# Output projection of a streaming trunk layer: branch sums on VectorE, branch tiles in another order, transposes of m sooner

## The chip, the cores and the metric

The kernel runs on one core of a Trainium2 chip. Its engines are TensorE (PE, the matmuls; PEld is its weight load), VectorE (DVE), ScalarE (ACT), GpSimd (POOL) and SyncE (SP, which issues most loads and stores). Each engine works through its own list of instructions in order, and waits on semaphores for the others. The metric is the device time of one execution, in microseconds (us). The kernel before took 2628.94, 2624.07 and 2617.74 us in three runs, so its median is 2624.07 us.

## The reference

One layer over 2048 rows of 1024 values. All of it is in float32.

```python
xn = rmsnorm(x, norm1_g)
u_pool, zq, zf, zi, zo, zg = split(xn @ w_in)            # 512 wide each, zg 2 x 1024
gates  = sigmoid(zg + b_gate).reshape(B, S, 2, 1024)
ya     = pool_mixer(u_pool, pool_w, pool_scale) @ w_pa   # branch "pa": 512 -> 1024
yb     = hgrn2_mixer(zq, zf, zi, zo, ...) @ w_pb         # branch "pb": 512 -> 1024
merged = gates[:, :, 0] * ya + gates[:, :, 1] * yb
x      = x + merged @ w_o                                # output projection: 1024 -> 1024
x      = x + (silu(gate) * value) @ w_down               # value, gate = conv(rmsnorm(x, norm2_g) @ w_up)
out    = rmsnorm(x, final_g)
```

## The kernel before

**Numbers and tiles.** Every matrix product is made in three matmuls: each operand is split into a rounded part hi and a rest lo (`split`: a cast to hi on ACT at L597, the difference lo on DVE at L598; weights likewise at L205 and L206), and hi*hi, hi*lo and lo*hi are added in PSUM. A tile is 128 x 512. There are 77 such places in SBUF for everything but weights, and 8 banks of PSUM.

**Seven products for eight.** The large products (input projection, output projection "wo", up projection, down projection "dn") take two blocks of 512 rows and two halves of the other dimensions together and use seven products P1 to P7 of sums and differences in place of eight. The two blocks are called the first rows (hf 0) and the second rows (hf 1) here; 1024 rows make a pass, and the program has two passes. The sums and differences of the input of a product are its forms: P1, P2 and P4 take a block as it is, P7, P5, P6 and P3 need a subtraction or an addition each.

**A pass.** In a pass come, on PE: the input projection, with the two mixers as background tasks; branch "pa"; branch "pb"; the output projection; the up projection; the down projection.

**The two branches.** `branch` goes through eight column tiles m in the order M_ORDER = (0, 4, 1, 5, 2, 6, 3, 7). For each m it fetches the gate tiles of m and the next two, gets the weights, and runs one chain of 12 matmuls of 128 x 512 for the first rows and then one for the second rows. In "pa" the inputs are `mixed` (tiles mx0_k of the first rows and mx1_k of the second, k = 0..3), loaded from DRAM by SP at L796 and split by a task; in "pb" they are `oT` (tiles oT0_k and oT1_k). After a chain `evac_a` multiplies the result with its gate on DVE into `ya`; `evac_b` does so into `gl` (L1285 for second rows, L1287 for first rows) and adds `gl` to `ya` on POOL (L1295). When m is 4 or more and the chain was that of the second rows, all four blocks of k = m - 4 are there, and `add_forms` makes the four forms P7, P5, P6, P3 of that k on POOL (L1084) into `yf`. That is 16 additions and 16 forms on POOL in a pass.

**The output projection.** `Rows.run` works through the products in the order P1, P6, P5, P7, P4, P3, P2, with four steps k each (the last steps of some are taken together), and 12 matmuls a step. `make` splits the forms, LEAD = 5 steps ahead of the step that uses them; the first five splits are therefore asked for when P1 begins. Products alternate between two groups of four banks, A and B: P1 and P5 use the same group A, so P5 waits until the 16 additions of P1's results into x (DVE, L1060) have read it.

**Forms of m.** The result x is called m as the input of the up projection. `forms_of("m")` starts two tasks: the first rows are normalised and transposed on PE at once; the second rows are normalised (L640) at once, but their transposes (L646) and the forms made of them (T2, T1, T3, T4; L703, L597, L598) wait until `go_up` is set. `ffn` sets it at the head of the up projection's unit number GO_AT = 5. The up projection begins with four units of P1, P1, P2, P2 for tiles 0 and 1, four more of the same kind for tiles 2 and 3, and then P6, the first that needs T2.

**What sets the order.** Weights come through `Stream`: raw tiles in 8 buffers (SP, L182), converted to `ops` up to four ahead. A raw load is queued on SP where the program reaches it and waits there for its buffer, and what is queued on SP behind it waits too. After every six matmuls `tick` advances the stream and the tasks by a step, so that background work is interleaved with PE's. The program text gives an order; a scheduler that simulates the engines then chooses the final order of each engine's list.

Of the kernel before, what the change touches and what calls it, by code (L numbers as in the profile page):

```python
# [15 lines left out]
ALU = mybir.AluOpType  # L16
AX = mybir.AxisListType

P = 128
SEQ = 2048  # L20
D = 1024
KD = D // P
# [24 lines left out]
OUT = R_OUT, R_OUT_BANK, R_OUT_NEW, R_OUT_ADD  # L47
# [10 lines left out]
M_ORDER = (0, 4, 1, 5, 2, 6, 3, 7)  # L58
# [1 line left out]
N_SLOTS = 77  # L60
N_RUN = 3
N_HEADS = 2
GO_AT = 5
LEAD = 5
X_AT, X_AT2 = 1, 4
GO_IO = (("P2", 1), ("P2", 0))
# [12 lines left out]
def tile_trunk(  # L79
# [16 lines left out]
    pe, act, dve, pool, sp = nc.tensor, nc.scalar, nc.vector, nc.gpsimd, nc.sync  # L96
# [9 lines left out]
    def slot(name, cols=TB, dt=F32):  # L106
        return slots.tile([P, cols], dt, tag="s", name=name, padded_shape=[P, 528])

    def bank(name, cols=512):
        return banks.tile([P, cols], F32, tag="b", name=name, padded_shape=[P, 512])  # L110
# [33 lines left out]
    def mm(*args, **kw):  # L144
        count[1] = pe.matmul(*args, **kw)  # L145
        count[0] += 1
        if count[0] % MM_PER_TICK == 0:
            tick()
# [102 lines left out]
    stream = Stream()  # L251
# [171 lines left out]
    def up_order():  # L423
        heads = [(0, 1), (2, 3), (4, 5)][:N_HEADS]
        res = [(m, p) for ms in heads for p in ("P1", "P2") for m in ms]
        res += [(m, p) for ms in heads for p in ("P6", "P5", "P7", "P4", "P3") for m in ms]

        rest = [(7 * m + 2 * i, m, p) for m in range(2 * N_HEADS, MF)
                for i, p in enumerate(ORDER)]
        return res + [(m, p) for _, m, p in sorted(rest)]  # L430
# [26 lines left out]
    sums = {}  # L457
# [39 lines left out]
    def load_x_tile(b, j):  # L497
        for c in range(2):
            t = slot(f"x{b}_{j}_{c}")
            r = b * TB + j * P  # L500
            sp.dma_start(t, x[r : r + P, 512 * c : 512 * c + 512])
            xt[("x", b), j, c] = t
        ready.add((("x", b), j))
# [97 lines left out]
    def chain_t(ps, w_of, xs, start=True, stop=True):  # L601
        n = len(xs)
        for k in range(n):
            wh, wl = w_of(k)
            xh, xl = xs[k]
            mm(ps, wh, xh, start=start and k == 0, stop=False)
            mm(ps, wh, xl, start=False, stop=False)
            mm(ps, wl, xh, start=False, stop=stop and k == n - 1)
# [185 lines left out]
    def fetch(d, name, eng=sp):  # L794
        t = slot(name)
        eng.dma_start(t, d)  # L796
        return t
# [277 lines left out]
                        step(j, k, ws[n])  # L1075
                stream.used(hold)

    def add_forms(two, forms, k, name, store=lambda p, t: None, sums=True, pin=lambda i: None):

        def comb(p, x0, x1, op):  # L1080
            if (p, k) in forms or x0 is None or x1 is None:
                return
            t = slot(f"{name}_{p}_{k}")
            pin(pool.tensor_tensor(t, x0, x1, op))  # L1084
            forms[p, k] = t
            store(p, t)

        for p, at in (("P1", (1, 0)), ("P2", (1, 1)), ("P4", (0, 1))):
            if (p, k) not in forms and at in two:
                forms[p, k] = two[at]  # L1090
                store(p, two[at])
        if not sums:
            return
        comb("P7", two.get((1, 0)), two.get((0, 0)), ALU.subtract)
        comb("P5", two.get((0, 0)), two.get((0, 1)), ALU.subtract)
        comb("P6", forms.get(("P5", k)), two.get((1, 0)), ALU.subtract)
        comb("P3", forms.get(("P6", k)), two.get((1, 1)), ALU.add)
# [54 lines left out]
    def mixer(b0, forms, late):  # L1152
# [90 lines left out]
        def gate(s, m, hf):  # L1243
            if (s, m, hf) not in gates:
                gates[s, m, hf] = fetch(gd[s, m, hf], f"gl{b0 + hf}_{s}_{m}")
            return gates[s, m, hf]
# [8 lines left out]
        mixed, oT = {}, {}  # L1255
# [8 lines left out]
                    mtask = Task(pa_task())  # L1264

        def branch(key, s, xs, evac, each):
            for n, m in enumerate(M_ORDER):
                each(n)
                for m2 in M_ORDER[n : n + 3]:
                    for hf in range(2):  # L1270
                        gate(s, m2, hf)
                w4 = stream.get(key)
                for hf in range(2):
                    ps = bank(f"{key}{b0 + hf}_{m}")
                    chain_t(ps, lambda k: (w4[:, 0, k * P : (k + 1) * P],
                                           w4[:, 1, k * P : (k + 1) * P]),
                            [xs[hf, k] for k in range(4)])
                    evac(m, hf, gate(s, m, hf), ps)
                stream.used(1)

        y, yf = {}, {}

        def gated(t, hf, g, ps):
            if hf:
                dve.scalar_tensor_tensor(t, g, -1.0, ps, ALU.mult, ALU.mult)  # L1285
            else:
                dve.tensor_tensor(t, g, ps, ALU.mult)  # L1287
# [4 lines left out]

        def evac_b(m, hf, g, ps):
            gated(g, hf, g, ps)
            pool.tensor_tensor(y[m, hf], y[m, hf], g, ALU.add)  # L1295
            if m >= KD // 2 and hf:
                k = m - KD // 2
                two = {(h, r): y[k + r * (KD // 2), h] for h in range(2) for r in range(2)}
                add_forms(two, yf, k, f"yf{b0}")

        join(mtask)
        otask = []
# [1 line left out]
        def start_o(n):  # L1304
            if n == O_AT:
                otask.append(Task(halves_task(od, range(HEADS), oT, "oT", O_LAG)))

        branch("pa", 0, mixed, evac_a, start_o)
        while any(t.live for t in runners):
            for t in runners:  # L1310
# [4 lines left out]
        acc = {}  # L1315

        def load_res(n):
            hf, j = n // NT, n % NT
            load_x_tile(b0 + hf, j)
            for c in range(2):  # L1320
                acc[hf, j, c] = xt.pop((("x", b0 + hf), j, c))

        branch("pb", 1, oT, evac_b, load_res)

        def ready_rows(hf):
            def done(j):
# [2 lines left out]
                ready.add((("m", b0 + hf), j))  # L1329
            return done  # L1330

        wo = Rows(f"wo{b0}", "wo", OUT, KD // 2, lambda p, k: yf[p, k], acc)
        go_up[0] = False
        for p in ("P1", "P6", "P5"):
            wo.run(p)
# [10 lines left out]
    def ffn(b0, forms, late):  # L1346
# [15 lines left out]
        def emit_up(m):  # L1362
# [17 lines left out]
            def glu(hf):  # L1380
                g = ts[1, hf]
                in_turn(act.activation(g, g, AF.Silu))  # L1382
                if hf:
                    dve.scalar_tensor_tensor(g, g, -1.0, ts[0, hf], ALU.mult, ALU.mult)  # L1384
                else:
                    (pool if m < G_POOL else dve).tensor_tensor(g, g, ts[0, hf], ALU.mult)
                k = m // 2
                two = gp.setdefault(k, {})
                two[hf, m % 2] = g

                def store(p, t):
# [69 lines left out]
        for n, (m, p) in enumerate(up_order()):  # L1461
            if n == GO_AT:
                go_up[0] = True
# [119 lines left out]
```

## Time and profile before

| what | value |
| --- | --- |
| runs | 2628.94, 2624.07, 2617.74 us (median 2624.07) |
| profiled execution | 2626.91 us, span 2625.2 us, mean granted TensorE clock 0.987 |
| PE busy | 2537.5 us (97%) |
| DVE busy | 1977.9 us (75%) |
| ACT busy | 1170.8 us (45%) |
| POOL busy | 913.0 us (35%) |
| POOL: L1295, 32 additions of ya and gl | 46.8 us, mean 1490 ns |
| POOL: L1084 into yf, 32 forms | median 1460 and 1458 ns |

The profile is one execution. PE is busy for 97% of the span, so what an edit can bring lies in the places where PE waits and in those where its granted clock (PEclk, a share of full speed) is low. The view of waits on PE lists them by what PE waited for: total us, how many times, and the longest. The view of windows gives the busy us of each engine in a stretch of time, with the granted clock. In both passes the branch "pb" runs beside POOL's additions; in the first pass "pa" begins at about 490 us and "pb" at 541 us, the output projection at 592 us, the up projection at 683 us; the output projection of the second pass begins at 1873 us.

### The profile page before, as it was taken

The numbers are of one execution on the slowest core, as the hardware profiler recorded it, in microseconds if no ns is written. First come the engines' busy times: TensorE is split into PE (matmuls) and PEld (weight loads), VectorE is DVE, ScalarE is ACT, GpSimd is POOL, SyncE is SP. The second block draws the span as 40 slices with busy tenths as digits, with TensorE's granted clock in tenths as the row PEclk, the third lists the DMA queues.
The fourth block names the chain that finished last, engine by engine and source line by source line (L and its number), as shares of the span: only waits on it lengthen the run. The fifth ranks groups of instructions, "written<-read, shape, count | busy, mean of one in ns | idle before, by whom it ended". The sixth has DMA issues, their size and how long they took to land. (4 is left out here: it accounts for less than half of the span.)

```text
span 2625.2 us, 35598 instructions
## 1 busy us (share of the span) xinstructions
PE 2537.5 (97%) x11464; PEld 2065.1 (79%) x11464; DVE 1977.9 (75%) x3390; ACT 1170.8 (45%) x2204; POOL 913.0 (35%) x1253
## 2 busy tenths in 40 slices
PE   7899999998999999999999999999999999999998
PEld 6688877777778888878878788888787888887887
DVE  7888779458789877877376787775778887777845
ACT  5334334313655454455364344443345454444633
POOL 6544344042444433353141111210623433335402
PEclk8999999999999999999999999999999999999999
DMA  6787759988768897488364344346452444445942
GB/s 213 271 223 205 204 181 245 267 263 209 217 184 244 239 235 211 148 299 282 98 206 159 97 125 133 109 153 213 149 166 88 151 151 148 141 140 182 378 142 105
DMA packets 254059, 496.90 MB, mean 189 GB/s; under 512 B 26736, under 2 KB 43248, under 8 KB 253552
## 3 DMA queue, kind: packets, MB, share of 16 engines
q1 hardware_dynamic: 187968, 319.89, 38.3%
q0 software_dynamic: 41504, 110.64, 16.5%
q10 hardware_dynamic: 24400, 64.08, 7.0%
q8 instruction: 91, 1.49, 0.2%
q14 instruction: 96, 0.79, 0.1%
HBM read 384.94 MB, written 187.17 MB: 218 GB/s over the span
## 5 line engine op out<-in xcount | busy, mean ns | idle before, releaser
L205 ACT CAST ops<-raw 128x512 fp32r<-128x512 f32 x732 | 451.5, 620 | 819.7 <-PE dn_P L145 140.0
L206 DVE TENSOR_TENSOR ops<-raw,ops 128x512 fp32r<-128x512 f32 x732 | 565.2, 776 | 205.3 <-ACT ops L205 194.3
L1375 DVE SCALAR_TENSOR_TENSOR e<-h,cols,e 128x512 f32<-128x512 f32 x176 | 142.6, 813 | 30.2 <-ACT e L1373 26.1
L1373 ACT ACTIVATE e<-h,cols 128x512 f32<-128x512 f32 x176 | 142.5, 814 | 24.2 <-DVE h L978 16.9
L1378 DVE SCALAR_TENSOR_TENSOR e<-h,cols,e 128x512 f32<-128x512 f32 x176 | 133.9, 769 | 3.0
L796 POOL DMA_DIRECT2D g_P<-dg_P x154 | 83.7, 545 | 107.6 <-PE dn_P L145 69.4
L1084 POOL TENSOR_TENSOR gf_P<-e,e 128x512 f32<-128x512 f32 x44 | 67.9, 1545 | 152.9 <-DVE e L1384 97.5
L1295 POOL TENSOR_TENSOR ya<-ya,gl 128x512 f32<-128x512 f32 x32 | 46.8, 1490 | 107.7 <-DVE gl L1287 107.7
L1084 POOL TENSOR_TENSOR gf_P<-gf_P,e 128x512 f32<-128x512 f32 x44 | 60.2, 1368 | 68.0 <-DVE e L1384 67.5
L1368 POOL COPY h<-h 128x2 f32<-128x2 f32 x88 | 40.7, 481 | 114.3 <-DVE h L976 112.3
L1370 POOL COPY hist<-h 128x2 f32<-128x2 f32 x88 | 35.3, 401 | 125.9 <-DVE h L978 124.2
L1382 ACT ACTIVATE e<-e 128x512 f32<-128x512 f32 x88 | 55.6, 631 | 38.8 <-DVE e L1378 38.4
L1191 POOL TENSOR_TENSOR q<-q,qs 128x512 f32<-128x512 f32 x16 | 21.9, 1366 | 141.6 <-ACT qs L1190 72.9
L978 DVE TENSOR_TENSOR h<-up_u,up_V 128x512 f32<-128x512 f32 x88 | 60.1, 684 | 13.6 <-PE up_V L145 13.1
L1228 ACT ACTIVATE gt<-gt,cols 128x512 f32<-128x512 f32 x48 | 34.8, 725 | 77.4 <-DVE gt L978 63.5
L845 POOL COPY qm<-q 128x64 f32<-128x64 f32 x64 | 24.9, 410 | 117.3 <-DVE q L910 31.2
L1060 DVE TENSOR_TENSOR x<-x,wo_P 128x512 f32<-128x512 f32 x88 | 56.6, 689 | 8.2 <-PE wo_P L145 8.2
L1060 DVE TENSOR_TENSOR ac<-ac,dn_P 128x512 f32<-128x512 f32 x72 | 46.6, 684 | 13.4 <-PE dn_P L145 13.3
L1398 POOL DMA_DIRECT2D dg_P<-gf_P x88 | 52.5, 596 | 10.8 <-POOL gf_P L1084 6.5
L853 PE MATMUL pl<-qm,k 128*128 128x192 f32 x256 | 48.2, 331 | 6.1 <-DVE qm L849 3.8
L1444 POOL TENSOR_TENSOR fss<-fss 128x1 f32<-128x1 f32 x16 | 4.6, 288 | 142.0 <-ACT fj L1433 142.0
L853 PEld LDWEIGHTS pl<-qm,k 128*128 128x128 f32 x256 | 43.3, 191 | 10.4 <-ACT qm L844 3.4
(1265 smaller groups left out, 8283.6 us busy)
## 6 DMA issues: line engine op xcount, KB each, us to landing
g_P<-dg_P POOLq DMA_DIRECT2D x154, 256.0 KB, 6.4
raw<-in_w_up_t SPq DMA_DIRECT2D x132, 256.0 KB, 3.2
raw<-in_w_in_t SPq DMA_DIRECT2D x98, 256.0 KB, 3.2
dg_P<-gf_P POOLq DMA_DIRECT2D x88, 256.0 KB, 3.9
raw<-in_w_io SPq DMA_DIRECT2D x68, 256.0 KB, 5.1
dg_P<-e SPq DMA_DIRECT2D x66, 256.0 KB, 3.3
raw<-in_w_dn SPq DMA_DIRECT2D x66, 256.0 KB, 3.0
x<-in_x SPq DMA_DIRECT2D x64, 256.0 KB, 5.3
```

The lines of the kernel that those rows point to most:

```text
L205: self.mark = act.copy(hi, v)
L206: dve.tensor_tensor(lo, v, f32(hi), ALU.subtract)
L796: eng.dma_start(t, d)
L853: pe.matmul(pa_[:, c * 192 : c * 192 + 192], ks[:, (i + c) * P : (i + c + 1) * P], mv[:, c].rearrange("p s x -> p (s x)"), start=True, sto ...
L978: dve.tensor_tensor(dst, t, ps, ALU.add if how == "add" else ALU.subtract)
L1060: dve.tensor_tensor(t, t, ps[j], ALU.add if sg > 0 else ALU.subtract)
L1084: pin(pool.tensor_tensor(t, x0, x1, op))
L1373: in_turn(act.activation(t, h[:, 2:], AF.Identity, bias=col(o_cb + mt), scale=col(o_cw + 4 * MF + mt)))
L1375: in_turn(second(dve.scalar_tensor_tensor(t, h[:, 1 : 1 + TB], col(o_cw + 2 * MF + mt), t, ALU.mult, ALU.add)))
L1378: dve.scalar_tensor_tensor(t, h[:, 0:TB], col(o_cw + mt), t, ALU.mult, ALU.add)
L1382: in_turn(act.activation(g, g, AF.Silu))
L1398: pool.dma_start(d, t)
```

## The change

Four edits:

1. GO_AT goes from 5 to 3, so that the transposes of the second rows of m are let go two units of the up projection sooner.
2. `add_forms` takes the engine as an argument, and `evac_b` uses DVE for the addition of `gl` to `ya` and for the four forms. The 16 + 16 operations of a pass go from POOL to DVE. Other callers of `add_forms` keep POOL.
3. `branch` begins with the first rows of the first two tiles (m = 0, 4), then the second rows of these two, and goes on as before. It holds two weight tiles meanwhile.
4. The Rows object of the output projection is created before branch "pb", and at tiles 3, 5 and 7 of "pb" its first, second and third split (P1, k = 0, 1, 2) are made.

```diff
-GO_AT = 5
+GO_AT = 3
...
-    def add_forms(two, forms, k, name, store=lambda p, t: None, sums=True, pin=lambda i: None):
+    def add_forms(two, forms, k, name, store=lambda p, t: None, sums=True, pin=lambda i: None,
+                  eng=pool):
...
-            pin(pool.tensor_tensor(t, x0, x1, op))
+            pin(eng.tensor_tensor(t, x0, x1, op))
...
         def branch(key, s, xs, evac, each):
-            for n, m in enumerate(M_ORDER):
-                each(n)
-                for m2 in M_ORDER[n : n + 3]:
-                    for hf in range(2):
-                        gate(s, m2, hf)
-                w4 = stream.get(key)
+            ws = {}
+
+            def chain(n, hf):
+                m = M_ORDER[n]
+                if n not in ws:
+                    each(n)
+                    for m2 in M_ORDER[n : n + 3]:
+                        for h in range(2):
+                            gate(s, m2, h)
+                    ws[n] = stream.get(key)
+                w4 = ws[n]
+                ps = bank(f"{key}{b0 + hf}_{m}")
+                chain_t(ps, lambda k: (w4[:, 0, k * P : (k + 1) * P],
+                                       w4[:, 1, k * P : (k + 1) * P]),
+                        [xs[hf, k] for k in range(4)])
+                evac(m, hf, gate(s, m, hf), ps)
+                if hf:
+                    stream.used(1)
+
+
+            for hf in range(2):
+                for n in range(2):
+                    chain(n, hf)
+            for n in range(2, len(M_ORDER)):
                 for hf in range(2):
-                    ps = bank(f"{key}{b0 + hf}_{m}")
...
-                    evac(m, hf, gate(s, m, hf), ps)
-                stream.used(1)
+                    chain(n, hf)
...
         def evac_b(m, hf, g, ps):
             gated(g, hf, g, ps)
-            pool.tensor_tensor(y[m, hf], y[m, hf], g, ALU.add)
+            dve.tensor_tensor(y[m, hf], y[m, hf], g, ALU.add)
             if m >= KD // 2 and hf:
...
-                add_forms(two, yf, k, f"yf{b0}")
+                add_forms(two, yf, k, f"yf{b0}", eng=dve)
...
-        branch("pb", 1, oT, evac_b, load_res)
+        wo = Rows(f"wo{b0}", "wo", OUT, KD // 2, lambda p, k: yf[p, k], acc)
+
+        def each_b(n):
+            load_res(n)
+            if n in (3, 5, 7):
+                wo.make(n // 2)
+
+        branch("pb", 1, oT, evac_b, each_b)
...
-        wo = Rows(f"wo{b0}", "wo", OUT, KD // 2, lambda p, k: yf[p, k], acc)
```

The lines move: L1285, L1287 and L1295 become L1299, L1301 and L1309, and L1084 becomes L1085. How the lists of the engines change shows at three places.

SP in the first pass, between the input projection and branch "pa". mx1_k are the tiles of the second rows, raw125 and raw126 loads of weights. Before:

```order
L796 DMA mx1_0_4864<-md1_0_2260 128x512
L182 DMA raw125_4966<-in_w_pb_t 128x512
L796 DMA mx1_1_4892<-md1_1_2420 128x512
L182 DMA raw126_5020<-in_w_pb_t 128x512
L796 DMA mx1_2_4932<-md1_2_4085 128x512
L796 DMA mx1_3_4938<-md1_3_4203 128x512
```

After:

```order
L796 DMA mx1_0_4864<-md1_0_2260 128x512
L796 DMA mx1_1_4892<-md1_1_2420 128x512
L182 DMA raw125_4966<-in_w_pb_t 128x512
L796 DMA mx1_2_4932<-md1_2_4085 128x512
L182 DMA raw126_4991<-in_w_pb_t 128x512
L796 DMA mx1_3_4938<-md1_3_4203 128x512
```

mx1_1 and mx1_2 each stand ahead of one more weight load; mx1_3 is where it was.

DVE in the first pass, from the last gate of branch "pb" to the first splits of the output projection (ya is the sum of the branches, yf its forms, wo_P_k the splits of a product's step k). Before:

```order
L1287 TENSOR_TENSOR gl_1_7_5586<-gl_1_7_5586,pb_7_5677 128x512
L1285 SCALAR_TENSOR_TENSOR gl_1_7_5588<-gl_1_7_5588,pb_7_5697 128x512
L206 TENSOR_TENSOR ops_5772<-raw_5410,ops_5772 128x512
L598 TENSOR_TENSOR wo_P_0l<-ya_0_5004,wo_P_0h 128x512
L598 TENSOR_TENSOR wo_P_1l<-ya_1_5092,wo_P_1h 128x512
L598 TENSOR_TENSOR wo_P_2l<-ya_2_5195,wo_P_2h 128x512
L598 TENSOR_TENSOR wo_P_3l<-ya_3_5294,wo_P_3h 128x512
L598 TENSOR_TENSOR wo_P_0l<-yf_P_0_5439,wo_P_0h 128x512
```

After:

```order
L1299 SCALAR_TENSOR_TENSOR gl_1_7_5596<-gl_1_7_5596,pb_7_5709 128x512
L206 TENSOR_TENSOR ops_5772<-raw_5390,ops_5772 128x512
L1309 TENSOR_TENSOR ya_7_5319<-ya_7_5319,gl_1_7_5594 128x512
L1309 TENSOR_TENSOR ya_7_5334<-ya_7_5334,gl_1_7_5596 128x512
L206 TENSOR_TENSOR ops_5793<-raw_5461,ops_5793 128x512
L1085 TENSOR_TENSOR yf_P_3_5727<-ya_3_5279,ya_7_5319 128x512
L1085 TENSOR_TENSOR yf_P_3_5729<-yf_P_3_5727,ya_3_5294 128x512
L206 TENSOR_TENSOR ops_5818<-raw_5509,ops_5818 128x512
L1085 TENSOR_TENSOR yf_P_3_5731<-yf_P_3_5729,ya_7_5334 128x512
L598 TENSOR_TENSOR wo_P_3l<-ya_3_5294,wo_P_3h 128x512
L598 TENSOR_TENSOR wo_P_0l<-yf_P_0_5439,wo_P_0h 128x512
```

The splits of P1's steps 0 to 2 are no longer here (they stand in "pb"), and the additions and forms stand ahead of that of step 3.

PE in the first pass, where the transposes of the second rows of m (m_t) come in the up projection. Before, in the middle of the unit P1 of tile 3, the sixth unit of the stage:

```order
L145 MATMUL up_3_X<-m_f1h,ops_6616 128x512
L145 MATMUL up_3_X<-m_f1l,ops_6616 128x512
L145 MATMUL up_3_X<-m_f1h,ops_6616 128x512
L646 MATMUL m_t_6700<-ident,m_xs_0_6459 128x128
L646 MATMUL m_t_6700<-ident,m_xs_0_6509 128x128
L646 MATMUL m_t_6700<-ident,m_xs_0_6542 128x128
L646 MATMUL m_t_6700<-ident,m_xs_0_6581 128x128
```

After, behind the unit P1 of tile 1, the second unit:

```order
L145 MATMUL up_1_X<-m_f3l,ops_6420 128x512
L145 MATMUL up_1_X<-m_f3h,ops_6420 128x512
L646 MATMUL m_t_6660<-ident,m_xs_0_6459 128x128
L646 MATMUL m_t_6660<-ident,m_xs_0_6509 128x128
L646 MATMUL m_t_6665<-ident,m_xs_1_6460 128x128
L646 MATMUL m_t_6665<-ident,m_xs_1_6510 128x128
L646 MATMUL m_t_6688<-ident,m_xs_0_6459 128x128
```

The transposes begin three and a half units sooner, with two of the four row tiles first; the last of the four row tiles comes behind the third unit for the first two columns of tiles, and behind the fourth for the next two.

More of the change, by code (lines that the diff above doesn't have):

```diff
@@ L1266, in branch @@
         def branch(key, s, xs, evac, each):
-            for n, m in enumerate(M_ORDER):
-                each(n)
-                for m2 in M_ORDER[n : n + 3]:
-                    for hf in range(2):
-                        gate(s, m2, hf)
-                w4 = stream.get(key)
-                for hf in range(2):
-                    ps = bank(f"{key}{b0 + hf}_{m}")
-                    chain_t(ps, lambda k: (w4[:, 0, k * P : (k + 1) * P],
-                                           w4[:, 1, k * P : (k + 1) * P]),
-                            [xs[hf, k] for k in range(4)])
-                    evac(m, hf, gate(s, m, hf), ps)
-                stream.used(1)
+            ws = {}
[19 more added lines that the diff above has]
+            for n in range(2, len(M_ORDER)):
+                for hf in range(2):
+                    chain(n, hf)
         y, yf = {}, {}
```

## The prediction, on record before the result was known

> **What bounds the kernel now.** I read the engines' shares first, then the waits on PE, then the windows around the longest of these waits, and last the timelines of the engine that PE waited for.
>
> ```profile
> span 2625.2 us, 35598 instructions
> PE 2537.5 (97%) x11464; PEld 2065.1 (79%) x11464; DVE 1977.9 (75%) x3390; ACT 1170.8 (45%) x2204; POOL 913.0 (35%) x1253
> ```
>
> PE is the bound: only the 88 us in which it does nothing can go, and the time it loses at a low clock. Of the waits on PE these lie in the stages that the change touches (total us, how many, the longest):
>
> ```profile
> PE wo_P L145 <- DVE wo_P_0l L598: 7.3, 2, 6.7
> PE pa L145 <- ACT mxs_1h L597: 6.3, 1, 6.3
> ...
> PE up_Z L145 <- ACT m_T23h L597: 3.7, 2, 1.8
> ...
> PE wo_P L145 <- DVE x L1060: 3.0, 2, 1.6
> ...
> PE wo_P L145 <- ACT wo_P_0h L597: 2.5, 2, 1.2
> ...
> PE pb L145 <- ACT oTs_0h L597: 1.7, 1, 1.7
> ...
> PE up_Z L145 <- DVE m_T23l L598: 1.5, 2, 0.8
> PE up_Z L145 <- ACT ops L205: 1.5, 2, 0.8
> PE up_V L145 <- DVE m_T12l L598: 1.4, 2, 0.7
> ...
> PE pb L145 <- ACT oTs_1h L597: 1.0, 1, 1.0
> ...
> PE up_Z L145 <- DVE up_u L1018: 0.9, 2, 0.5
> ...
> PE up_Z L145 <- DVE m_T43l L598: 0.5, 2, 0.2
> ...
> PE pb L145 <- DVE oTs_1l L598: 0.2, 1, 0.2
> PE pb L145 <- DVE oTs_0l L598: 0.2, 1, 0.2
> ```
>
> That is 6.3 us for pa, 3.1 for pb, 12.8 for wo and 9.5 for up, 31.7 in all. The waits of pa and pb come once, in the first pass; those of wo and up in both. The windows behind the longer ones add a loss (columns: the stretch, its length, busy us of PE, PEld, DVE, ACT, POOL with instructions, granted clock, DMA share, GB/s):
>
> ```profile
> 490.00:496.40 6.40, 0.05 (x2) 0.05 (x1) 0.07 (x1) 0.72 (x3) 0.00 (x0) 0.85 1.03 395
> 496.40:501.30 4.90, 4.90 (x12) 3.49 (x13) 3.10 (x8) 2.80 (x11) 3.59 (x4) 0.50 1.01 351
> 543.50:554.91 11.41, 8.25 (x25) 5.62 (x25) 6.17 (x10) 2.47 (x4) 0.00 (x0) 0.85 0.97 351
> 545.30:548.80 3.50, 2.01 (x5) 0.96 (x6) 1.72 (x3) 1.24 (x3) 0.00 (x0) 1.00 0.92 322
> 548.80:552.00 3.20, 3.20 (x9) 2.32 (x9) 3.20 (x7) 0.62 (x1) 0.00 (x0) 0.54 1.06 405
> 592.00:602.00 10.00, 3.06 (x10) 2.25 (x11) 10.00 (x3) 3.34 (x7) 9.92 (x8) 0.74 0.93 208
> 601.00:605.50 4.50, 4.47 (x11) 3.51 (x12) 4.50 (x5) 3.36 (x7) 4.42 (x4) 0.50 0.57 172
> 605.50:610.00 4.50, 4.50 (x18) 3.60 (x17) 4.50 (x9) 2.54 (x5) 0.55 (x1) 0.82 1.06 153
> ```
>
> Behind the pa wait the clock is 0.50 for 4.90 us, 2.45 us lost. Behind the long wo wait it is 0.50 and then 0.82 for 4.50 us each, 2.25 + 0.81 = 3.1 us lost. In pb it falls to 0.54 behind small waits.
>
> **A. The pa wait (first pass).** What PE waited for, by the timelines of SP and ACT, and the price of a chain of 12 matmuls, from the chain of waits:
>
> ```profile
> 486.14 0.33 SPq L182 DMA_DIRECT2D raw<-in_w_pb_t  x1
> 486.57 0.91 SPq L796 DMA_DIRECT2D mx<-md  x1
> ...
> 495.68 0.62 ACT L597 CAST mxs_1h<-mx 128x512 fp32r<-128x512 f32 x1 [6.90 <-DMA mx<-md]
> ...
> 2393.37 2.79 PE up_Z L145 x12
> ```
>
> The load of mx1_1 stood on SP behind a weight load that waited for its buffer until 486.14, landed nine us later, and its cast ended the wait. The change does two things. The chain of the second rows starts one chain later, 2.79 us. And mx1_1 and mx1_2 each stand ahead of one weight load; mx1_3 does not. Removable: 6.3 + 2.45 = 8.8. Lower bound: the moved chain alone, 2.8. The DMA share is 1.03 while PE waits, so I leave a wait of 2.5 us for the later tiles, about one chain. Whether it costs clock too is open: in pb waits of 1.7 and 1.0 were followed by 3.20 us at 0.54 (1.5 lost), so A is 8.8 − 2.5 = 6.3 without that and 4.8 with it. I take 5.5.
>
> The Trainium skill ("TensorE: Matmul & The Clock Gate", section "What's actually happening") says that the clock falls after an idle window of about 3.4 us. By that alone the remaining wait would cost no clock, A would be 6.3 and the sum 0.8 higher. The pb windows disagree in this kernel: PE was busy 2.01 of the 3.50 us ahead of the 0.54.
>
> **B. The pb start (first pass).** From 543.50 to 554.91 PE did two chains, 5.6 us of work, in 11.4: 5.8 removable, more than the 3.1 of waits.
>
> ```profile
> 536.73 0.32 SPq L182 DMA_DIRECT2D raw<-sw0s  x1
> ...
> 538.11 0.59 SPq L796 DMA_DIRECT2D oT<-od  x1
> ...
> 544.69 0.62 ACT L597 CAST oTs_0h<-oT 128x512 fp32r<-128x512 f32 x1 [3.16 <-DMA oT<-od]
> ```
>
> Here too the second rows now begin a chain later, and on SP oT1_0 stands ahead of the weight load that was issued at 536.73 only; oT1_2 and oT1_3 still stand behind the next. Bounds 2.8 (the chain alone) and 5.8; I take 4.0, since two of four tiles move.
>
> **C. The start of wo (both passes).** DVE and POOL at that place (the first three rows from DVE's timeline, the last from the tile's view: min/median/max ns):
>
> ```profile
> 592.52 8.45 DVE L598 TENSOR_TENSOR wo_P_0l<-ya,wo_P_0h 128x512 fp32r<-128x512 f32 x1
> 600.90 1.76 DVE L598 TENSOR_TENSOR wo_P_1l<-ya,wo_P_1h 128x512 fp32r<-128x512 f32 x1
> ...
> 1891.99 2.47 DVE L1060 TENSOR_TENSOR x<-x,wo_P 128x512 f32<-128x512 f32 x4
> ...
> L1295 POOL TENSOR_TENSOR ya<-ya,gl x32: 1281/1300/1784, 557.2 to 1877.9; 128x512 f32<-128x512 f32 x32
> ```
>
> A DVE difference took 8.45 us while POOL worked off its sums (POOL was busy 9.92 of 10 us), and 1.76 beside a POOL operation; with POOL idle four additions took 2.47, 0.62 each. After the change nothing of this runs on POOL, and three of the first four splits are done earlier. Removable: 12.8 + 3.1 = 15.9. What does DVE pay? In pb a pair of chains takes PE 5.6 us. Beside it DVE has two gates, two additions, one weight difference, in every second pair four forms, and some splits: 7 operations a pair on average, 4.3 us at 0.62. That is hidden by PE. Behind the last chain, at T0, stand ten operations up to the split of wo_P_3 (the order above): 6.2 us, and P1's fourth step begins 3 × 2.79 = 8.4 after T0. P5 begins eight steps, 22.3, after T0 and needs P1's 16 additions; DVE has 33 operations until then, 20.5 us. Both fit with some 2 us over, so the waits for x (3.0) should go too. I take 14.5 of 15.9, the rest for weight loads and casts that come between. Lower bound: only the DVE-bound wait goes, 7.3, and clock and other waits stay.
>
> **D and E. The transposes sooner, the up stage (both passes).** The weight loads of the stage's first products (first and last start), and DVE's timeline in the first pass:
>
> ```profile
> L145 PEld LDWEIGHTS up_X<-m_f0h,ops x88: 187/187/189, 683.1 to 2371.2; 128*128 128x128 f32 x88
> ...
> 689.46 1.07 DVE L640 TENSOR_SCALAR m_xs<-x,m_3r 128x512 f32<-128x512 f32 x2 [0.72 <-POOL m_3r L620]
> ...
> 699.17 0.75 DVE L703 SCALAR_TENSOR_TENSOR m_t<-m_t,cols,m_b 128x512 f32<-128x512 f32 x1
> ...
> 701.64 1.37 DVE L206 TENSOR_TENSOR ops<-raw,ops 128x512 fp32r<-128x512 f32 x1 [0.56 <-DMA raw<-su0s]
> ...
> 713.46 1.21 DVE L598 TENSOR_TENSOR m_T23l<-m_t,m_T23h 128x512 fp32r<-128x512 f32 x1 [0.68 <-ACT m_T23h L597]
> ```
>
> The chain for T2 runs from 699.17 to 714.67 and PE waits 1.8 + 0.8 = 2.6 at its end. Now the transposes come about two units (5.6 us) sooner. The last row tile is normalised at 690.5, and the third unit ends about 8.4 after the stage's begin at 683.1, at 691.5, so they are not waited for. The T2 waits go: 3.7 + 1.5 = 5.2, and of the waits behind them 0.4, so 5.6. T12, T43 and weight waits follow PE's own pace and stay. Bounds: half of it, 2.8, if the chain on DVE and ACT is slower beside more of P1's work; 9.5 if all waits go.
>
> **Sum.** 5.5 + 4.0 + 14.5 + 5.6 = 29.6. The profiled execution took 2626.9 and would take 2597.3; it lies 2.8 above the median of the runs, 2624.1, so the median is forecast at 2594.5. Upper bounds: 8.8 + 5.8 + 15.9 + 9.5 = 40.0, to 2584. Lower: 2.8 + 2.8 + 7.3 + 2.8 = 15.7, to 2608.4.
>
> **Rivals.**
>
> R1, slower: DVE becomes the bound of pb and wo. At a pitch of p us an operation a pass loses 8 × (7p − 5.6) in pb and 33p − 22.3 up to P5. It begins to cost above p = 0.68, cancels the gain of 29.6 at p = 0.92, and at p = 1.0 costs 21.9 a pass, 43.8: 2594.5 + 43.8 = 2638. For it: DVE is at 1.76 beside POOL, and waits on ACT come between. Against it: the 0.62 with POOL idle, and POOL's large work there is what moves. The Trainium skill ("Perfetto Trace Analysis", section "Optimizing Scalar/DVE Operations") advises to give work of a saturated DVE to ScalarE or GpSimd, which speaks against this change; the same section says that GpSimd and DVE share a read port of SBUF and moving between the two may not help. The 1.76 beside POOL bears out the second.
>
> R2, the loads are late wherever they stand on SP: A is 2.8 and B nothing. Gain 22.9, 2601. For it: DMA shares of 0.92 to 1.06 in these windows.
>
> R3, the sooner transposes bring nothing, because what T2 needs from POOL, ACT and PSUM is late as before. Gain 24.0, 2600.
>
> R4, no change that can be told: in the first pass PE reaches the up stage some 19 us sooner (5.5 + 4.0 + the first pass's part of C, about 10), and waits there for weight sums from DRAM (the row at 701.64 shows DVE waiting for su0s). Then only the second pass gains: C's waits without the first pass's 6.7 + 1.2 are 4.9, E's half 2.8; 7.7, 2616. Against it: the wait in that row is DVE's 0.56, not PE's, and loads by buffers follow PE's pace.
>
> **How the numbers follow.** The main case has 0.60, R2 and R3 together 0.20, R4 0.12, R1 0.08. I take 2584 for the lower end. For the upper I add to 2608.4 the 4.9 by which the slowest run lies over the median: 2613. That holds the main case, R2 and R3, 8 in 10. A measurement of this kernel can tell about 0.5% (13.1 us) from no change; a gain of under that is R4 alone. So faster 0.80, same 0.12, slower 0.08.
>
> **What the profile after would show.** A: the mxs wait of 6.3 shrinks to about 2.5 and the clock behind it stays above 0.50. B: the 11.4 us window shrinks to 7 or 8. C: no wait for wo_P_0l, none for x at P5, DVE differences of 0.6 to 0.7 at the start of wo, POOL idle there. E: L703 begins about 5.6 us sooner after the stage's begin and m_T23 is not waited for. Wrong it would be if DVE operations in pb take 1 us or more and wo waits for wo_P_3 or P5 for x for longer than before, or if new waits for weights stand at the start of up.

## The result, and the profile after

The time did not change: 2627.31 us (median of 22 runs, 2620.85 to 2634.17) against 2626.55 us before (22 runs, 2617.74 to 2631.26). The ratio is 1.0007, with an interval of 0.9998 to 1.0016. The forecast was 2594.5.

The page of the changed kernel, its first rows:

```profile
span 2630.4 us, 35554 instructions
PE 2542.7 (97%) x11464; PEld 2070.1 (79%) x11464; DVE 1983.0 (75%) x3454; ACT 1171.5 (45%) x2204; POOL 819.6 (31%) x1189
```

GpSimd lost 93 us of work (913.0 before). VectorE, with 64 instructions more, is busy only 5 us longer, because its other instructions got shorter. The edits did what they say. PE's waits in the stages that the change touches, in the changed kernel:

```profile
PE up_X L145 <- ACT up_e L1012: 9.5, 2, 4.8
...
PE pa L145 <- ACT mxs_2h L597: 3.5, 1, 3.5
...
PE wo_P L145 <- DVE wo_P_2l L598: 3.0, 1, 3.0
...
PE pb L145 <- ACT oTs_2h L597: 2.6, 1, 2.6
PE wo_P L145 <- DVE x L1060: 2.4, 2, 1.9
PE pt L962 <- DVE ot L956: 2.0, 1, 2.0
...
PE pa L145 <- ACT mxs_3h L597: 1.2, 1, 1.2
PE wo_P L145 <- DVE wo_P_3l L598: 1.0, 1, 1.0
PE wo_P L145 <- DVE wo_P_1l L598: 1.0, 1, 1.0
...
PE pb L145 <- DVE ya L1301: 0.7, 1, 0.7
```

Nearly every wait that the prediction wanted to remove is gone by name (mxs_1h, oTs_0h and 1h, wo_P_0l, m_T23h and l), and another stands in its place: a later tile of the same load, a later split, and one that is new, up_e with 9.5 us.

Where the time went shows by stage. The table has the time from the first matmul of a stage to the first of the next, read from PE's timeline of each profiled execution. The stretch ahead of pa does the same work in all kernels, and still differs by up to 8 us between executions (475.6 to 483.6), so stages are compared here, and not single spans. The last three columns are experiments told below; the two with the sums held have GO_AT = 5.

| stage | before | changed | sums held from pb | sums held from pa | the best kernel |
| --- | --- | --- | --- | --- | --- |
| pa, pass 1 | 61.1 | 62.9 | 61.0 | 56.2 | 53.4 |
| pb, pass 1 | 51.6 | 50.8 | 46.7 | 44.4 | 44.4 |
| wo, pass 1 | 91.0 | 90.4 | 81.7 | 81.5 | 81.5 |
| up, pass 1 | 438.0 | 440.8 | 440.8 | 439.4 | 434.7 |
| pb, pass 2 | 46.0 | 44.5 | 44.4 | 44.4 | 44.6 |
| wo, pass 2 | 85.8 | 81.7 | 81.7 | 81.7 | 81.5 |
| up, pass 2 | 438.8 | 442.7 | 440.5 | 439.5 | 433.9 |

In the second pass pb and wo gain 5.6 us, as forecast. In the first pass the same edits gain 1.4, and pa loses 1.8. The up projection loses in both. How much is not firm: over the runs with GO_AT = 5 one execution of this stage takes 437.3 to 440.8 us. What is firm there are the waits.

**What GpSimd did with its time.** In the first pass a background task builds sums of the up weights in DRAM (`Sums.make`, L275 on GpSimd and L278 on ACT): tiles su1s, su2s and so on, by transfers of 1024 KB, of which GpSimd's add to what is there. GpSimd's timeline before, in branch pb and the begin of wo:

```profile
580.31 1.14 POOL L275 DMA_DIRECT2D su3s<-in_w_up_t  x1
591.88 1.13 POOL L275 DMA_DIRECT2D su4s<-in_w_up_t  x1
603.74 1.14 POOL L275 DMA_DIRECT2D su3s<-in_w_up_t  x1
604.38 1.66 POOL L275 DMA_DIRECT2D su4s<-in_w_up_t  x1
```

The same after:

```profile
541.96 1.16 POOL L275 DMA_DIRECT2D su3s<-in_w_up_t  x1 [38.28 <-DMA su3s<-in_w_up_t]
558.55 1.15 POOL L275 DMA_DIRECT2D su4s<-in_w_up_t  x1 [15.44 <-DMA su4s<-in_w_up_t]
573.69 1.15 POOL L275 DMA_DIRECT2D su3s<-in_w_up_t  x1 [13.99 <-DMA su3s<-in_w_up_t]
576.15 1.15 POOL L275 DMA_DIRECT2D su4s<-in_w_up_t  x1 [1.31 <-DMA su4s<-in_w_up_t]
```

Before, these issues stood on GpSimd between its slow sums and were issued at 580 to 604. After, each waits for nothing but the transfer ahead of it, and all four are out by 576. What the queues moved between 541 and 597 us, in the view of DMA (the software queue is GpSimd's), before:

```profile
q0 software_dynamic: 697, 1.39, 14.1%
...
gl<-gd SPq DMA_DIRECT2D x16, 256.0 KB, 5.0
...
su3s<-in_w_up_t POOLq DMA_DIRECT2D x1, 1024.0 KB, 11.0
```

and after:

```profile
q0 software_dynamic: 2112, 4.19, 41.8%
...
gl<-gd SPq DMA_DIRECT2D x14, 256.0 KB, 5.9
...
su3s<-in_w_up_t POOLq DMA_DIRECT2D x2, 1024.0 KB, 12.9
```

Three times the bytes of this queue fall into these 56 us, which are pb and some 5 us beside it, and with them the DMA share of the whole of pb rises (windows over that stage, before and after; the last but one number is the DMA share):

```profile
540.70:592.30 51.60, 47.21 (x194) 36.80 (x192) 33.45 (x35) 8.67 (x15) 33.78 (x26) 0.97 0.86 275
```

```profile
546.50:597.30 50.80, 47.11 (x193) 36.87 (x192) 26.98 (x44) 8.48 (x14) 3.44 (x3) 0.97 1.06 294
```

The gates come late for it. VectorE's timeline of the changed kernel:

```profile
591.32 0.69 DVE L1301 TENSOR_TENSOR gl<-gl,pb 128x512 f32<-128x512 f32 x1 [9.59 <-DMA gl<-gd]
591.92 1.29 DVE L1085 TENSOR_TENSOR yf_P<-ya,ya 128x512 f32<-128x512 f32 x2
...
607.00 0.69 DVE L598 TENSOR_TENSOR wo_P_2l<-ya,wo_P_2h 128x512 fp32r<-128x512 f32 x1
```

VectorE has less than one operation every microsecond to do in pb and does each in 0.6 us, but it stands still for 9.59 us for a gate, and when wo begins at 597 it has six of the sixteen gates of pb still ahead of it. SP's queue shows the same from its side: SP waited 12.8 us in one piece for a transfer of su3s (8.6 before) with gate loads queued behind:

```profile
SPq L796 <- DMA su3s<-in_w_up_t: 12.8, 1, 12.8
```

The gate load that waits here reads nothing of su3s. In the trace it waits on a semaphore that ACT's copy into su3s had used before it; that copy was issued at 560.72 and landed at 573.14, and the load was issued at 573.15. Eight semaphores go round among the loads of SP and the transfers of ACT. So a slow transfer makes loads late in two ways, through its share of the DMA engines and by holding up SP's list. No run below tells the two apart.

**The transposes.** ACT's and PE's timelines of the changed kernel, where P2 of tile 2 begins in the up projection:

```profile
711.64 0.62 ACT L597 CAST m_T23h<-m_t 128x512 fp32r<-128x512 f32 x1 [2.16 <-DVE m_t L703]
712.17 0.58 ACT L1012 COPY up_e<-up_X 128x512 f32<-128x512 f32 x1
...
713.16 0.59 ACT L1012 COPY up_e<-up_X 128x512 f32<-128x512 f32 x1
```

```profile
712.80 0.79 PE L145 MATMUL up_X<-m_f4h,ops 128*128 128x512 f32 x1 [4.75 <-ACT up_e L1012]
```

Before, ACT's copies for the same two tiles, 2 and 3, stood ahead of the first cast of T2 and behind the second:

```profile
697.34 0.59 ACT L1012 COPY up_e<-up_X 128x512 f32<-128x512 f32 x1 [1.66 <-PE up_X L145]
...
705.16 0.62 ACT L597 CAST m_T21h<-m_t 128x512 fp32r<-128x512 f32 x1 [2.44 <-DVE m_t L703]
705.68 0.58 ACT L1012 COPY up_e<-up_X 128x512 f32<-128x512 f32 x1
```

P2 writes into the bank of PSUM from which ACT copies P1's result (L1012). In the changed kernel PE had that result of tile 2 ready at about 705. The copy stands on ACT behind the cast of m_T23, and that waits 2.16 us for VectorE. The T2 chain does end sooner, and what it displaced on ACT holds PE up for longer than the wait that it removed.

### The profile page after: what moved, and what is told of

Read it like the earlier page. It is cut to its first block, busy times and chain, and to the rows that moved or that the text cites. A ratio compares the mean times of both kernels' runs of the same rounds, so it can differ in the third digit from the quotient of the medians.

```text
span 2630.4 us, 35554 instructions
## 1 busy us (share of the span) xinstructions
PE 2542.7 (97%) x11464; PEld 2070.1 (79%) x11464; DVE 1983.0 (75%) x3454; ACT 1171.5 (45%) x2204; POOL 819.6 (31%) x1189
## 4 chain that ended last, share of the span: by engine, by line
PE 70%; DVE 1%; ACT 1%; issue 1%; DMA 0%; POOL 0%; DVEq 0%; POOLq 0%; ACTq 0%
PE dn_P L145 16%; PE up_Z L145 14%; PE up_V L145 9%; PE up_X L145 9%; PE wo_P L145 3%; PE gr_Z L145 3%; PE pa L145 2%; PE gr_V L145 2%; PE pb L145 2%; PE gr_X L145 2%; PE io_Z L145 1%; PE fr_Z L145 1%; PE fr_X L145 1%; PE fr_V L145 1%; PE io_V L145 1%; PE pl L853 1%
## 5 line engine op out<-in xcount | busy, mean ns | idle before, releaser
L206 DVE TENSOR_TENSOR ops<-raw,ops 128x512 fp32r<-128x512 f32 x732 | 548.7, 753 | 189.0 <-ACT ops L205 182.3
L1085 POOL TENSOR_TENSOR gf_P<-e,e 128x512 f32<-128x512 f32 x44 | 67.8, 1542 | 152.9 <-DVE e L1404 97.5
L1085 POOL TENSOR_TENSOR gf_P<-gf_P,e 128x512 f32<-128x512 f32 x44 | 60.2, 1367 | 68.7 <-DVE e L1404 68.3
L1060 DVE TENSOR_TENSOR ac<-ac,dn_P 128x512 f32<-128x512 f32 x72 | 46.7, 682 | 13.3 <-PE dn_P L145 13.2
L1012 ACT COPY up_e<-up_X 128x512 f32<-128x512 f32 x44 | 25.8, 586 | 53.0 <-PE up_X L145 47.9
```

The source lines that it names most:

```text
L206: dve.tensor_tensor(lo, v, f32(hi), ALU.subtract)
L1060: dve.tensor_tensor(t, t, ps[j], ALU.add if sg > 0 else ALU.subtract)
L1085: pin(eng.tensor_tensor(t, x0, x1, op))
```

## The experiments

Theory L: freed of its sums, GpSimd starts the weight sums' transfers sooner, and they delay the loads of pa and pb. Theory U: the sooner transposes put the copies of up_X behind the casts of T2. The rival of the first is that VectorE has too much to do by itself (the prediction's R1). Each ratio is to runs of the kernel before that were timed in the same set. Experiments of different sets are compared by their medians; the medians of before in the sets lie between 2623.9 and 2626.0 us, so such a difference can be off by some 2 us.

**GO_AT back to 5** in the changed kernel.

```diff
-GO_AT = 3
+GO_AT = 5
```

> The changed kernel with GO_AT back at 5, all else as changed. Theory U (the sooner transposes cost time): in the changed kernel PE waits 4.75 us in each pass for the copy of up_X (L1012), which stands on ACT behind the casts of T2; from the begin of the up projection to that of the down projection it took 440.8 and 442.7 us where the kernel before took 438.0 and 438.8. So that wait goes, the waits of 1.8 and 0.8 us for m_T23 come back, the stage takes 438 to 439 us again, and the kernel is 6.7 us faster than the changed one: about 6 us faster than before. Rival (the up stage is longer for another reason, such as weights that come late after the earlier stages): the stage stays at 441 us or more and the time within 2 us of the changed kernel's.

Measured: 2626.37 us (11 runs), ratio to before 1.0004 (0.9994 to 1.0014). The wait for up_e is gone and those for m_T23 are back (3.7 and 1.5), as expected; the up stages take 440.2 and 439.8 us. The expected gain of 6.7 did not come: against the changed kernel it is 0.9 us, no more than the intervals leave open. In the profiled execution the up stages are 0.6 and 2.9 us shorter than in the changed kernel, but pa and wo of the first pass are 0.8 and 2.6 us longer. So this run alone does not decide for theory U.

**GO_AT = 3 alone**, on the kernel before.

```diff
-GO_AT = 5
+GO_AT = 3
```

> The kernel before with GO_AT = 3 and nothing else. Theory U: the same wait of 4.75 us for up_X's copy appears twice, the waits for m_T23 go, and the kernel is 6 to 7 us slower than before. The prediction's own step (5.6 us faster) should show the m_T23 waits gone and nothing in their place.

Measured: 2632.97 us, ratio 1.0026 (1.0015 to 1.0037), 8 us slower than before in the same comparison (2624.94). The 9.5 us of waits for up_e come, and m_T23 is not waited for. The sign is that of theory U, and the prediction's step is refuted.

**The sums alone on VectorE**, on the kernel before.

```diff
-            pool.tensor_tensor(y[m, hf], y[m, hf], g, ALU.add)
+            dve.tensor_tensor(y[m, hf], y[m, hf], g, ALU.add)
...
-                add_forms(two, yf, k, f"yf{b0}")
+                add_forms(two, yf, k, f"yf{b0}", eng=dve)
```

> The kernel before with only the branch additions and the forms on VectorE. Theory L: the first pass gains little, since its transfers come sooner here too (begin of pb to begin of up 140 to 143 us, 142.6 before), and the second pass gains 4 to 6 us (131.8 before): 4 to 7 us faster in all. The prediction's term C would give 10 to 14.

Measured: 2634.46 us, ratio 1.0036 (1.0022 to 1.0050): 9.5 us slower, where 4 to 7 faster was expected. The second pass gained 4.2 us in wo, but pb of the first pass took 59.3 us, 7.7 more than before, by this wait of PE:

```profile
PE pb L145 <- ACT oTs_0h L597: 8.0, 1, 8.0
```

with two of GpSimd's issues just ahead of it:

```profile
535.90 1.16 POOL L275 DMA_DIRECT2D su3s<-in_w_up_t  x1 [34.59 <-DMA su3s<-in_w_up_t]
...
542.04 1.15 POOL L275 DMA_DIRECT2D su4s<-in_w_up_t  x1 [4.98 <-DMA su4s<-in_w_up_t]
```

The expectation missed the sign of the whole. It is not only the gates that come late, but the input of pb: its load, issued at 538.47, landed 12.8 us later, where the same load before took 6.6. At the begin of wo PE waited 8.0 us for wo_P_0l, no less than before (6.7), and VectorE had stood still for 5.76 and 4.89 us for gates ahead of it.

**The weight sums held in pb.** The changed kernel with GO_AT = 5, where the task waits 24 ticks (of six matmuls) more at the begin of pb. VectorE does the moved sums as in the changed kernel.

```diff
+        if b0 == 0:
+            prep[0].wait += 24
         branch("pb", 1, oT, evac_b, each_b)
```

> The changed kernel with GO_AT = 5 and with the task that builds the sums of the up weights in DRAM held for 24 ticks (33 us) at the begin of branch pb of the first pass; the moved sums stay on VectorE. Theory L (GpSimd, freed of its sums, starts these transfers 30 to 40 us sooner, and they take the DMA engines from the gates' loads): the DMA share in pb falls from 1.0 to 1.1 to about 0.8, VectorE's waits for gates (9.6 us the longest) go to under 3, PE's waits for wo_P_1l, 2l, 3l (5.0 us) go, and the kernel is 6 to 10 us faster than with GO_AT = 5 alone. Rival V (VectorE has too much to do in pb and wo by itself): the waits for wo_P stay, and the time is that of GO_AT = 5 alone, within 2 us.

Measured: 2613.07 us, ratio 0.9949 (0.9937 to 0.9962), 13 us less than with GO_AT = 5 alone in the same comparison. No wait for wo_P is left, SP waits for no weight sum in pb any more, and wo takes 81.7 us in the first pass as in the second. The window over pb:

```profile
543.20:589.90 46.70, 45.22 (x193) 35.75 (x192) 38.27 (x63) 8.39 (x14) 1.15 (x1) 1.00 0.87 271
```

VectorE does more in this stage than in the changed kernel (38.27 us against 26.98) and the stage is shorter. So it is not VectorE's work that filled the first pass (the rival), but the transfers that came sooner: theory L holds. By which of the two ways the loads were late, the run does not tell.

**The weight sums held from pa on**, GO_AT = 5.

```diff
+        if b0 == 0:
+            prep[0].wait += 60
         branch("pa", 0, mixed, evac_a, start_o)
```

> As the run with the hold in branch pb (changed kernel, GO_AT = 5), but the task of the weight sums is held for 60 ticks from the begin of branch pa on. Theory L says that the waits for mx1_2 and mx1_3 in pa (3.1 and 1.2 us with the hold in pb) come from the same contention: su1 and su2 are copied and added from 490 to 520 us, at DMA shares of 1.1. Then pa takes 54 to 56 us in place of 61.0, the gain of pb and wo stays, and the kernel is 5 to 7 us faster than with the hold in pb: 2606 to 2608. Rival (these tiles are late because they still stand behind weight loads on SP, which wait for buffers that PE's pace frees): pa stays at 60 to 61 us and the time at 2613.

Measured: 2601.85 us, ratio 0.9907 (0.9893 to 0.9922). PE waits for no mxs and no oTs any more; what is left in pa is one wait of 2.43 us for a transpose of the mixer. The loads of mx1_2 and mx1_3 land after 4.4 and 3.9 us, where they took 9.5 and 10.0 in the changed kernel. So the first-row order was not what pa lacked: su1 and su2 took the DMA engines there, in the kernel before too.

**The new order of the branches alone**, on the kernel before.

```diff
-            for n, m in enumerate(M_ORDER):
...
+            for hf in range(2):
+                for n in range(2):
+                    chain(n, hf)
```

> The kernel before with only the new order of the chains in the branches. The prediction gave A + B = 9.5 us. What the profiles show so far says that pa stays at 60 to 61 us, since mx1_2 and mx1_3 stand behind the same weight loads and land nine to ten us after they are issued, with the wait moved from mxs_1h to mxs_2h and mxs_3h; and that pb's begin gains 2 to 4 us, with GpSimd's sums as before. So the first pass's pa and pb together 109 to 111 us (112.7 before).

Measured: 2623.85 us in one run. pa takes 63.7 us and pb 48.8, together 112.5 (112.7 before). In pa the wait of 6.3 us has become 2.92 (mxs_2h), 1.96 (mxs_3h) and 2.04 (a transpose), and pa is 2.6 us longer; pb gained 2.8. The sum stayed above the 109 to 111 us expected.

**The old order, with the weight sums held**, in pb and then from pa on (GO_AT = 5, sums on VectorE, early splits).

```diff
-            for hf in range(2):
-                for n in range(2):
-                    chain(n, hf)
...
+            for n, m in enumerate(M_ORDER):
```

> As the run with the hold in branch pb, but the branches in the old order of their chains. It tells what the new order (the prediction's A and B) is worth where the moved sums no longer bring transfers forward. In pa the new order changed nothing that could be seen (61.0 against 61.1 us); at the begin of pb the second rows needed a chain later should be worth 2 to 4 us. So 2 to 4 us slower than with the hold in pb, by a longer pb in the first pass (49 to 51 us in place of 46.7). The prediction's A + B would make it 9 to 10 us slower.

> The run with the hold from branch pa on and GO_AT = 5, with the branches in the old order of chains. It tells what the new order is worth with the loads free of the sums. If mx1_1 still comes late because it stands behind a weight load on SP, pa is 59 to 61 us (56.2 with the new order) and the kernel 3 to 6 us slower than 2601.85; if the transfers alone were the cause, pa stays at 56 and the time within 2 us.

Measured: held in pb 2608.22 us, ratio 0.9930 (0.9912 to 0.9949); held from pa on 2599.54 us, ratio 0.9901 (0.9888 to 0.9915). In neither is the old order slower than the new (0.9949 and 0.9907). The first expectation was wrong; of the second, the case of the transfers alone comes nearest. In pa it takes 53.5 us against 56.2, with a wait of 0.71 us for mxs_1h. With the loads in time the new order is worth nothing, and it may cost some 2 us.

**The hold alone**, on the kernel before.

```diff
+        if b0 == 0:
+            prep[0].wait += 60
         branch("pa", 0, mixed, evac_a, start_o)
```

> The kernel before, with the weight sums held for 60 ticks from the begin of branch pa and nothing else. It tells how much of the 23 us is the hold's own. Theory L: pa gains about 4 to 6 us and pb's begin 3 to 5, since the loads come in time; the begin of wo stays as it was (91 us in the first pass, 86 in the second), since GpSimd's additions still keep VectorE and the forms late: 2615 to 2618. If the hold alone gave more than 15 us, the change's edits would be worth little.

Measured: 2613.15 us, ratio 0.9957 (0.9942 to 0.9972). pa takes 54.1 us, pb 45.8, wo 85.3 in the first pass and 86.0 in the second. This is more than expected: wo of the first pass, 91.0 before, was to stay as it was. So 12.9 us of the gain is the hold's own. The sums on VectorE and the early splits bring 13.6 on top of it (2599.54 with the old order), of which the first pass's wo gave 3.8, the second's 4.5, and pb 1.4 in each pass.

**GO_AT = 3 and 4, with the weight sums held from pa on** (the new order).

```diff
-GO_AT = 5
+GO_AT = 3
```

> The changed kernel as it is (GO_AT = 3) with the weight sums held for 60 ticks from the begin of branch pa. Against the run with the same hold and GO_AT = 5 (2601.85 us) only the transposes of m differ. Theory U: 9.5 us of waits for up_X's copy come, 5.2 of waits for m_T23 go; 3 to 6 us slower, 2605 to 2608. The prediction's step would make it 5.6 us faster, 2596.

```diff
-GO_AT = 5
+GO_AT = 4
```

> The same with GO_AT = 4. Theory U: the copies of up_X are again behind the casts of T2, or the m_T23 waits shrink; between the two, 2599 to 2606.

Measured: 2607.21 us (0.9926, 0.9912 to 0.9940) and 2608.56 us (0.9940, 0.9925 to 0.9954), 5.4 and 6.7 us more than with 5, of which the interval of the first just overlaps that of 5 (0.9893 to 0.9922). Both wait for up_e twice, by 4.4 to 4.8 us. The second lies above the 2599 to 2606 that were expected.

**No early splits** (old order, hold from pa on, GO_AT = 5).

```diff
-            if n in (3, 5, 7):
-                wo.make(n // 2)
```

> Old order of the branches, sums on VectorE, weight sums held from branch pa on, GO_AT = 5, but without the three splits of P1 made during branch pb. VectorE then has four splits to make when wo begins, 0.6 us each, behind the last additions, and PE waits for the first of them: 1.2 us of ACT and 1 to 2 us of VectorE in each pass; 3 to 6 us slower than 2599.54. If the moved sums alone are the gain, within 2 us of it.

Measured: 2604.96 us, ratio 0.9917 (0.9903 to 0.9930), 5.4 us more than with the splits, with intervals that overlap a little. PE waits 1.29 and 1.23 us for the first cast of wo, and pb, which ends there, is longer by 1.4 and 1.3 us. So the splits are 3 to 5 of the 13.6 us, and the moved sums the rest. This run also makes the plainest pair for theory L. The moved sums in the old order, without early splits, made the kernel 9.5 us slower where the weight sums were free (2634.46 against 2624.94), and make it some 8 us faster where they are held (2604.96 against 2613.15).

**The steps of T2 spread out.** Old order, hold from pa on, GO_AT = 3; the four steps of T2 are asked for at every second tick, or every third.

```diff
             full["T2"].append(t2)
-            yield 1
+            yield 2 if src[0] == "m" else 1
```

> Old order of the branches, sums on VectorE, weight sums held from branch pa on, GO_AT = 3, and the four steps of the T2 forms asked for at every second tick in place of every tick, so that on ACT the copies of up_X for tiles 2 and 3 stand behind the casts of T21 and T22 in place of all four. Theory U (the place of these copies on ACT is what makes the sooner transposes cost time): the wait of 4.5 to 4.8 us for the copy shrinks to under 2 and m_T23 is not waited for; 2594 to 2599, up to 5 us faster than the same with GO_AT = 5 (2599.54). Rival (the wait is for a bank of PSUM that the transposes hold, not for the place on ACT): the wait stays at 4 us or more and the time is 2603 to 2606.

> The same with the steps of T2 at every third tick: both copies stand ahead of the cast of T22. Theory U: no wait for the copies; T2 itself is later, so m_T23 may be waited for again by 1 to 3 us; 2594 to 2600. Rival as in the run with every second tick: 2603 to 2606.

Measured: 2589.91 us (0.9864, 0.9851 to 0.9878) with two ticks and 2592.44 us (0.9879, 0.9865 to 0.9892) with three. Neither waits for up_e or m_T23. The copies now stand between the casts on ACT (two ticks):

```profile
677.23 0.62 ACT L597 CAST m_T21h<-m_t 128x512 fp32r<-128x512 f32 x1
677.75 0.58 ACT L1012 COPY up_e<-up_X 128x512 f32<-128x512 f32 x1
...
680.87 0.62 ACT L597 CAST m_T22h<-m_t 128x512 fp32r<-128x512 f32 x1
681.39 0.58 ACT L1012 COPY up_e<-up_X 128x512 f32<-128x512 f32 x1
...
684.86 0.62 ACT L597 CAST m_T23h<-m_t 128x512 fp32r<-128x512 f32 x1 [0.25 <-DVE m_t L703]
```

So the sooner transposes do bring what the prediction expected of them and more (9.6 us against 2599.54), when the copies that PE waits for are not put behind them. One thing the two runs do not separate: with the steps, three of the four pairs of transposes also come some matmuls later, and so take their PSUM banks later. That the copy's place on ACT was the cause rests on the rows of the changed kernel, where the copy begins as the cast of m_T23 ends. The steps were not spread with GO_AT = 5.

The kernel with two ticks is the best of all: 2589.9 us, 1.36% under before.

## Why the prediction was wrong

- **What bounds the kernel.** The list of waits was right, and most of them could be removed: the best kernel is 34 us faster than before, within the upper bound of 40. It needed two edits that the change does not have, the sums held and the steps of T2 spread.
- **C, the begin of wo: the step that failed.** "After the change nothing of this runs on POOL" was costed for VectorE alone. What GpSimd starts sooner was not asked, though its timeline has the weight sums' issues (L275) between the sums. The transfers moved up by 28 to 38 us into a stage whose DMA share was 0.86 already, and the gates that VectorE needs for the sums came late. B and C forecast 18.5 us for pb and wo; the two stages gained 7.0, of which 1.4 in the first pass. In the second pass, where no sums are built, C held (4.1 us in wo and 1.5 in pb, where the waits had been 4.9). In the first pass 9.3 us of wo came back once the transfers were held (81.7 against 91.0). VectorE's own count held: with the transfers held PE waits for no split and no addition of x, so R1 was rightly small. What C expected of the profile came true as well: at the begin of wo VectorE's operations take 0.69 us and GpSimd makes no sums. That was not enough.
- **A and B, the loads.** "Lower bound: the moved chain alone, 2.8" was no bound. It took the landing of the other tiles as fixed, and the wait moved on to mx1_2 and mx1_3, which took ten us to land (DMA share 0.99 from 495.5 to 505.5 us). The waits left in pa are 3.5, 1.2 and 2.0 us, no less than the 6.3 before, and the clock did fall to 0.50 behind them (505 to 510 us), which the prediction had as a sign of being right if it stayed above. R2 named the lateness of the loads and gave it the wrong price, A of 2.8; pa became 1.8 us longer. With the transfers held, pa gained 4.9 us in the new order and 7.5 in the old, and pb 7.2 in either (5.5 and 4.0 were forecast): the order is not what gained there. By itself, without the hold, it took 2.8 us off pb and put 2.6 on pa, in one run.
- **D and E, the transposes.** "The T2 waits go" was right, and L703 begins 6.0 us sooner after the stage's begin (5.6 forecast). What else stands on ACT's list among T2's casts was not asked. 5.2 us of waits went and 9.5 came. R3 had the gain at nothing; the price had the other sign: 0.9 to 8 us by the three pairs of kernels that differ in GO_AT alone (0.9 in the changed kernel, 5.4 with the sums held, 8.0 on the kernel before).
- **R4** gave the outcome, no change that can be told, but not the time (2616) nor the way: PE did not wait for weight sums at the begin of up, the making of these sums took the loads' time in pa and pb, some hundred us ahead of it. Of the 24.0 forecast for A, B and C, the run with the sums held from pa on shows 23.3, but 12.9 of it comes by the hold without any of the edits.
- **The chances.** R2 itself cited DMA shares of 0.92 to 1.06 in pa and pb. A case in which the transfers get worse, not just stay late, was missing.

## What to carry to other kernels

When work is taken off an engine, read what else stands on its queue: transfers that were held back by that work start sooner, and if the loads of the next stage are close to what the DMA engines carry, the gain goes there. Look too at what the late transfer holds up by order alone, as the load on SP's list that waited for a semaphore. A background task that is paced by an engine's slowness should be given its place on purpose. The same holds for a step that is moved up on an engine in order: look at what is queued behind it, above all copies that free a bank of PSUM for PE.

## What was not expected of the hardware

The same waits did not always cost the same. In the kernel with the old order and the sums held from pa on, the waits of 1.85 and 0.76 us for m_T23 were followed by a low clock (windows behind them: busy us of PE second, granted clock third from the end):

```profile
684.00:687.40 3.40, 1.55 (x7) 0.72 (x5) 2.72 (x5) 0.89 (x3) 0.85 (x2) 1.00 0.32 98
687.40:690.40 3.00, 2.24 (x5) 1.64 (x6) 2.29 (x3) 1.87 (x4) 3.00 (x5) 0.56 0.18 63
690.40:694.40 4.00, 4.00 (x11) 3.08 (x10) 3.11 (x3) 0.66 (x2) 1.96 (x2) 0.50 1.05 147
```

In the kernel before, the waits of 1.84 and 0.75 us at the same place left it at full speed:

```profile
709.00:713.00 4.00, 2.64 (x11) 1.58 (x9) 3.68 (x5) 1.49 (x4) 1.45 (x2) 1.00 0.76 164
713.00:717.00 4.00, 2.77 (x11) 2.08 (x12) 3.31 (x4) 3.06 (x6) 4.00 (x5) 1.00 0.22 68
```

The loss in the first, over PE's busy time, is 2.24 × 0.44 + 4.00 × 0.50 = 3.0 us, more than the waits themselves. It is one reason why the up stage gained 10 us from waits of some 5 us, and why the pairs that differ in GO_AT alone give 0.9 to 8 us; that it explains all of that spread is not shown.
